# RWKV value and output products over used token rows only, in 32-column array tiles

## The chip, the cores and the metric

The kernel runs on one core of a Trainium2 chip. The metric is the device time of one execution in microseconds (us). TensorE is called PE, its weight loads PEld, VectorE DVE, ScalarE ACT, GpSimd POOL; SP is the engine that issues the transfers.

## The reference

One layer of a hybrid decoder for a prompt of 256 tokens and 8 samples of 4 tokens each (288 columns in all, in fp32), width 2048. One input projection feeds a retention group (8 heads of 256) and an RWKV-7 group (32 heads of 64); both outputs go through one output projection, a gate and the residual, and a final RMSNorm. The change is in the RWKV group, whose recurrence for each head is

```
sa = S @ (-kk_t)
S  = S * w_t + outer(sa, kk_t * a_t) + outer(v_t, k_t)
o_t = S @ r_t
```

Each output `o_t` is normalised over the 64 values of its head, scaled and shifted, a bonus term is added, and the sum is multiplied by a SiLU gate. The state S at the end of the prompt and of each sample is an output too.

## The kernel before

**Order of the work.** The wide matmuls of the projections (tile `acc`, line 419 in `wblocks`) go to PE block by block; each weight block is split into a rounded part `whi` (ACT, line 383) and a remainder `wlo` (DVE or POOL, line 387), three blocks ahead. Everything else is written as generators. A planner at build time keeps an estimated clock for each engine (`account`, line 201, with costs from `c_pe`, `c_dve`, `c_act` and `c_pool`), and after every three wide matmuls `tick` (line 293) lets those generators go on whose inputs its clocks call ready. `flag` and `wait` (lines 322 and 325) order the generators among each other at build time; a generator that waits lets others go ahead of it. The result is one fixed order of instructions for each engine. All instructions of the helper class have line 255 in the profile, so they are told apart by their tiles.

**RWKV groups.** The 32 heads are worked off in 8 groups `q` of four heads: two pairs `p` of two heads `h`. The prompt is cut into 8 chunks of 32 tokens (`CH`), and the 32 sample tokens are a ninth chunk, c = 8. For each group `main_gen` (line 784) does, in this order:

- `AR` (line 806) and `BK` (lines 827 to 833): decayed and scaled rows; AR has the tag "AR" or "BK" in turn, and BK of the last group takes the tag "AR".
- the score product `scp` (line 855): four-tile matmuls `mm4` of 64 x 64, masked into `SC`. In SC, UV and XR the 64 partitions of a head are two halves of 32: in SC and UV the first half stands for the delta rows and the second for the value rows.
- the turn stage (`turn_gen`, line 930): transposes of BK, in which the second half of the tile `UV` serves as scratch, then copies into `BKt`.
- the values are transposed into rows 32 to 63 of each head's part of `UV` (lines 868 to 879).
- the value product `avp` (line 891): for each p, c and head one matmul of 32 rows and 64 columns into two PSUM tiles of the tag "ch" (which has two buffers) and a third for c = 8; ACT brings it into `XR` under the mask `amask` (lines 893 and 894).
- beside it `inv_gen` (line 952) inverts the chunk triangles, and then `chain_gen` (line 1011) goes through the 8 chunks one after the other, adding into XR and filling the first rows of UV; `sample_gen` (line 1077) does chunk 8.
- `out_gen` (line 1132): the output product `ops` (line 1142), 36 matmuls of 64 rows and 64 columns, is added to XR (lines 1145 and 1146); the output rows then stand in 32 of each 64 partitions. Then come 18 statistics instructions over all of XR (line 1151), small sums, a power on POOL (line 1162), subtraction and scaling (lines 1165 and 1169), copies that bring 32 x 32 blocks into place (ACT, lines 1173 and 1177) and a transpose into `on` (line 1179), flag "xr", and the last two steps into the rows `y` of the output projection's input, flag "rw".

An fp32 matmul is two instructions in the profile, one for each pass.

**The end.** After the last group's projections the output projection runs. Its input rows are split in pairs by `split_gen` (line 1502), which waits for "rw" of the last group before its ninth pair (line 1506); the blocks that use these pairs come at a fixed place in the order (line 1569), the first of them 22 blocks after the first output block.

Of the kernel before, what the change touches and what calls it, by code (L numbers as in the profile page):

```python
# [10 lines left out]
F32 = mybir.dt.float32  # L11
F32R = mybir.dt.float32r
AF = mybir.ActivationFunctionType
# [88 lines left out]
def tile_hybrid_step(  # L102
# [222 lines left out]
    def wait(*names):  # L325
        while not all(n in flags for n in names):
            yield
        cur[0].done["flag"] = max(flags[n] for n in names)
        yield
# [358 lines left out]
    def rwkv_blocks(q):  # L688
# [95 lines left out]
        def main_gen():  # L784
# [17 lines left out]
            yield  # L802
            yield from wait(("la", q))
            if q > 1:
                yield from wait(("ops", q - 2))
            ar = mx.tile([P, 2, 9, 2, CH], F32, tag="BK" if q % 2 else "AR", name="AR")
            AR = [ar[:, p] for p in range(2)]
            for p in range(2):
                ep, es = eps_[p]
                stt(AR[p][:, 0:8, 0, :], c9(kkn[p][:, 0:TP]), -1.0, ep[:, :, 0:32], MUL, MUL)  # L810
                stt(bb(AR[p][:, 8, 0, :]), bb(kkn[p][:, TP:NR]), -1.0, es[:, :, 0:4], MUL, MUL)
                yield
# [28 lines left out]
                yield from wait(("ops", q - 1))  # L841
            BKt = mx.tile([P, 2, 9, 64], F32, tag="BKt", name="BKt")
            SC = mx.tile([P, 2, 9, 64], F32, tag="SC", name="SC")
            UV = mx.tile([P, 2, 9, 64], F32, tag="UV", name="UV")
            B.update(AR=AR, BKt=BKt, SC=SC, UV=UV)
            mk = K("mwkv")
            flat = lambda t: t.rearrange("p a t -> p (a t)")
            yield PART
# [16 lines left out]
            spawn(bonus_gen(kps))  # L865
            vw = B["vw"]
            yield from wait(("turn", q))
            V.transpose(UV[:, 0, :, 32:64], c9(vw[:, 0, :]))
            yield
            for h in range(2):  # L870
# [11 lines left out]
            XR = mx.tile([P, 2, 9, 64], F32, tag="XR", name="XR")  # L882
            B["XR"] = XR
            yield PART
            avps, av8 = [pch.tile([P, 512], F32, tag="ch", name="avp") for p in range(2)], tps("avp")
            for p in range(2):
                for c in range(9):
                    for h in hs2:
                        v = slice(h.start + 32, h.stop)
                        t = avps[p][h, 64 * c:64 * c + 64] if c < 8 else av8[h, 64 * p:64 * p + 64]  # L890
                        mm(t, SC[v, p, c, :], UV[v, p, c, :])
            for p in range(2):
                act(XR[:, p, 0:8, :].rearrange("p c k -> p (c k)"), avps[p], AF.Copy, scale=K("amask"))
            act(XR[:, :, 8, :], av8[:, 0:128].rearrange("p (a k) -> p a k", a=2), AF.Copy, scale=K("amask"))
            yield from pace(SPC)
            yield from wait(("inv", q), ("bkt", q))
# [31 lines left out]
            flag(("bps", q))  # L928

        def turn_gen(BK, BKt):  # L930
            T2 = B["UV"][:, 1]
            for a in range(2):
                s = slice(32 * a, 32 * a + 32)
# [197 lines left out]

        def out_gen():
            SC, UV, XR = B["SC"], B["UV"], B["XR"]
            bst = rwp.tile([P, 18, 6], F32, tag="bst", name="bst")
            gst = rwp.tile([P, 3, 18], F32, tag="gst", name="gst")
            yield PART
            ops, op8 = [pch.tile([P, 512], F32, tag="ch", name="ops") for p in range(2)], tps("ops")
            for p in range(2):
                for c in range(9):
                    for h in hs2:  # L1140
                        t = ops[p][h, 64 * c:64 * c + 64] if c < 8 else op8[h, 64 * p:64 * p + 64]
                        mm(t, SC[h, p, c, :], UV[h, p, c, :])
            for p in range(2):
                xv = XR[:, p, 0:8, :].rearrange("p c k -> p (c k)")
                tt(V, xv, ops[p], xv, ADD)
            tt(V, XR[:, :, 8, :], op8[:, 0:128].rearrange("p (a k) -> p a k", a=2), XR[:, :, 8, :], ADD)
            yield from pace(SPC)
            flag(("ops", q))
            for p in range(2):
                for c in range(9):  # L1150
                    V.bn_stats(bst[:, 9 * p + c], XR[:, p, c, :])
                yield
            mean, dif, var = gst[:, 0], gst[:, 1], gst[:, 2]
            tt(V, mean, bst[:, :, 1], bst[:, :, 4], ADD)
# [4 lines left out]
            ts(V, mean, mean, 0.5, None, MUL)  # L1159
            yield  # L1160
            ts(G, var, var, 1.0 / 64, 64e-5, MUL, ADD)
            tt(G, var, var, nhalf[:, 0:18], ALU.pow)
            yield
            for p in range(2):
                tt(V, XR[:, p], XR[:, p], gst[:, 0, 9 * p:9 * p + 9].unsqueeze(2).to_broadcast([P, 9, 64]), SUB)
                yield
            for p in range(2):
                o = XR[:, p]
                tt(V, o, o, gst[:, 2, 9 * p:9 * p + 9].unsqueeze(2).to_broadcast([P, 9, 64]), MUL)
                on = rwp.tile([P, NR], F32, tag="on", name="on")  # L1170
                yield
                for h in range(2):
                    S.copy(o[quad(h, 0), :, 32 - 32 * p:64 - 32 * p], o[quad(h ^ p, 1), :, 0:32])
                yield
                if p == 1:
                    for h in range(2):
                        S.copy(o[quad(h, 1), :, 0:32], o[quad(1 - h, 1), :, 32:64])
                    yield
                V.transpose(c9(on), o[:, :, 32 - 32 * p:64 - 32 * p])
                yield  # L1180
                if p == 1:
                    flag(("xr", q))
                stt(on, on, lnw(p), yd(p), MUL, ADD)
                stt(yd(p), on, lnb(p), sg[:, p], ADD, MUL)
                yield
# [432 lines left out]
```

## Time and profile before

| | us |
|---|---|
| median of three runs | 1561.44 (1560.08 to 1562.62) |
| the profiled execution, its own time | 1563.12 |
| span of its instructions | 1561.3 |
| mean granted clock of PE | 0.973 |

The profile is one execution, taken by the hardware profiler. Its page gives busy time by engine, a groups view lists instructions of equal kind with their count, busy time and mean length, and a timeline has them in order of time; a line of the timeline with "x72" is 72 instructions merged, its length from the first start to the last end. "Idle before" is time in which the engine did nothing just before the instruction, and the name behind the arrow is what it then waited for.

### The profile page before, as it was taken

Reading aid. Unit: us, or ns where it says so; the run is one execution under the profiler, and the core shown is the slowest. Engines: PE = TensorE matmul, PEld = TensorE weight load, DVE = VectorE, ACT = ScalarE, POOL = GpSimd, SP = SyncE. Lnnn points to the kernel's source line nnn. Section 1 sums busy time; section 2 is a strip of 40 time slices with the busy share of each in tenths; the row PEclk is TensorE's granted clock in tenths of the full one; section 3 lists DMA queues with packets and bytes.
Section 4 is the critical chain, followed back from the end, with each engine's and each line's share of the span. In section 5 each row is a group of like instructions: output and inputs, shape, how many; then the busy total and the mean of one; then the engine's idle time right before and its main releaser. Section 6 shows DMA issues by size and latency. Waiting matters only on the chain. (4 is left out here: it accounts for less than half of the span.)

```text
span 1561.3 us, 37454 instructions
## 1 busy us (share of the span) xinstructions
PE 1463.4 (94%) x14194; PEld 1305.5 (84%) x14194; DVE 1165.6 (75%) x2889; ACT 778.4 (50%) x1698; POOL 462.4 (30%) x469
## 2 busy tenths in 40 slices
PE   4889999999999999899999999999999989999996
PEld 1668887888888878888888899879987977999996
DVE  2434787998788878967987799789878987855453
ACT  2224564464445644644555546545653554455443
POOL 0001322442343145323422353245243422202010
PEclk8889999999999999999999999999999999999998
DMA  9996654674476557645764566466536544675553
GB/s 286 341 347 213 196 156 129 183 195 146 126 240 193 146 146 220 189 119 154 216 182 137 154 180 174 114 170 179 155 101 182 159 133 111 193 237 167 158 162 115
DMA packets 347761, 277.30 MB, mean 178 GB/s; under 512 B 90270, under 2 KB 346110, under 8 KB 346868
## 3 DMA queue, kind: packets, MB, share of 16 engines
q1 hardware_dynamic: 347580, 274.91, 60.5%
q8 instruction: 111, 1.82, 0.5%
q14 instruction: 70, 0.57, 0.1%
HBM read 248.80 MB, written 26.03 MB: 176 GB/s over the span
## 5 line engine op out<-in xcount | busy, mean ns | idle before, releaser
L255 PE MATMUL acc<-Hhi,whi 128*128 128x288 f32 (+2 forms) x2080 | 618.6, 312 | 13.3 <-ACT whi L255 5.3
L255 PE MATMUL acc<-Hlo,whi 128*128 128x288 f32 (+2 forms) x2080 | 618.6, 309 | 0.0
L255 ACT CAST whi<-raw 128x512 fp32r<-128x512 f32 (+1 forms) x648 | 395.4, 618 | 353.0 <-PE acc L255 209.2
L255 POOL TENSOR_TENSOR wlo<-raw,whi 128x512 fp32r<-128x512 f32 x224 | 311.0, 1392 | 758.5 <-ACT whi L255 546.0
L255 PE MATMUL acc<-Hhi,wlo 128*128 128x288 f32 (+2 forms) x2080 | 458.5, 302 | 14.8 <-DVE wlo L255 13.9
L255 PEld LDWEIGHTS acc<-Hhi,whi 128*128 128x128 f32 (+1 forms) x2080 | 397.5, 191 | 42.7 <-issue 11.3
L255 PEld LDWEIGHTS acc<-Hlo,whi 128*128 128x128 f32 (+1 forms) x2080 | 398.4, 192 | 17.3 <-issue 8.1
L255 DVE TENSOR_TENSOR wlo<-raw,whi 128x512 fp32r<-128x512 f32 (+1 forms) x424 | 304.8, 724 | 121.7 <-ACT whi L255 117.0
L255 PEld LDWEIGHTS acc<-Hhi,wlo 128*128 128x128 f32 (+1 forms) x2080 | 340.5, 191 | 22.0 <-DVE wlo L255 19.7
L255 PE MATMUL acc<-ylo,whi 128*128 128x288 f32 x480 | 136.4, 298 | 0.7 <-DVE ylo L255 0.7
L255 PE MATMUL acc<-yhi,whi 128*128 128x288 f32 x480 | 135.9, 298 | 1.0 <-ACT whi L255 1.0
L255 PE MATMUL acc<-yhi,wlo 128*128 128x288 f32 x480 | 101.5, 297 | 0.1
L255 PEld LDWEIGHTS acc<-yhi,whi 128*128 128x128 f32 x480 | 90.4, 188 | 1.4 <-ACT whi L255 1.3
L255 PEld LDWEIGHTS acc<-ylo,whi 128*128 128x128 f32 x480 | 90.4, 188 | 1.3 <-DVE ylo L255 1.0
L255 PEld LDWEIGHTS acc<-yhi,wlo 128*128 128x128 f32 x480 | 76.3, 189 | 0.7 <-POOL wlo L255 0.3
L255 PE MATMUL adaps<-raw,cT 128*32 128x256 f32 x768 | 56.3, 409 | 7.8 <-DMA raw<-in_w_ada_dram 7.8
L255 DVE COPY UV<-ch 32x64 f32<-32x64 f32 x128 | 28.9, 225 | 29.1 <-ACT UV L255 26.1
L255 ACT COPY UV<-ch 32x64 f32<-32x64 f32 x128 | 25.5, 199 | 47.8 <-PE ch L255 46.0
L255 DVE SCALAR_TENSOR_TENSOR s0b<-s0b,ups 128x512 f32<-128x512 f32 x64 | 41.0, 681 | 9.0 <-PE ups L255 8.9
L255 PEld LDWEIGHTS adaps<-raw,cT 128*32 128x32 f32 x768 | 20.2, 114 | 30.4 <-DMA raw<-in_w_ada_dram 15.3
L255 POOL TENSOR_TENSOR rot<-rot,rt 128x288 f32<-128x288 f32 x32 | 29.1, 932 | 44.7 <-DVE rt L255 44.7
L255 DVE SCALAR_TENSOR_TENSOR S<-ch,dec,SP 128x64 f32<-128x64 f32 x112 | 30.5, 278 | 13.8 <-PE ch L255 12.7
(260 smaller groups left out, 1966.8 us busy)
## 6 DMA issues: line engine op xcount, KB each, us to landing
raw<-in_w_in_dram SPq DMA_DIRECT2D x512, 256.0 KB, 3.1
raw<-in_w_ada_dram SPq DMA_DIRECT2D x64, 512.0 KB, 8.3
raw<-in_w_out_dram SPq DMA_DIRECT2D x128, 256.0 KB, 3.0
raw<-in_w_ada_dram SPq DMA_DIRECT2D x64, 256.0 KB, 2.8
s0b<-in_state_ret_dram SPq DMA_DIRECT2D x64, 256.0 KB, 4.6
out_dram<-s0b SPq DMA_DIRECT2D x64, 256.0 KB, 3.2
y<-in_x_prompt_dram SPq DMA_DIRECT2D x4, 1024.0 KB, 6.6
s0r<-in_state_rwkv_dram SPq DMA_DIRECT2D x128, 32.0 KB, 2.8
```

What stands on the lines that cost most here:

```text
L255: return f(*a, **k)
```

## The change

The value product and the output product are computed for those 32 of 64 rows of each head that hold a result, so that every matmul writes 32 partitions in place of 64; the odd chunks are written into the neighbouring 32 columns of the array, and with that into the other 32 partitions of the head. The prompt chunks of one product fit in one "ch" tile in place of two. ACT brings the value product into XR with one copy for the odd and one for the even chunks (each under the mask), and two more that move the odd chunks' rows to their place. The sum of ops and XR goes into a new place `O`, the AR tile of the group (for group 6 the UV tile), in which 5 columns of 64 stand on all 128 partitions in place of 9: four pairs of chunks, and the sample chunk on one half. Statistics, power, subtraction and scaling run over these 10 columns instead of 18. Sixteen copies instead of six bring the blocks back into XR for the transpose.

The tiles' owners change with it: AR of group q waits for the flag "xr" of group q-2 in place of "ops"; UV is taken in `turn_gen` in place of `main_gen`, and in the last group only after "xr" of group 6.

```diff
--- before.py
+++ after.py
@@ -802,9 +802,10 @@
             yield
             yield from wait(("la", q))
             if q > 1:
-                yield from wait(("ops", q - 2))
+                yield from wait(("xr", q - 2))
             ar = mx.tile([P, 2, 9, 2, CH], F32, tag="BK" if q % 2 else "AR", name="AR")
             AR = [ar[:, p] for p in range(2)]
+            B["ar"] = ar
             for p in range(2):
                 ep, es = eps_[p]
                 stt(AR[p][:, 0:8, 0, :], c9(kkn[p][:, 0:TP]), -1.0, ep[:, :, 0:32], MUL, MUL)
@@ -841,8 +842,7 @@
                 yield from wait(("ops", q - 1))
             BKt = mx.tile([P, 2, 9, 64], F32, tag="BKt", name="BKt")
             SC = mx.tile([P, 2, 9, 64], F32, tag="SC", name="SC")
-            UV = mx.tile([P, 2, 9, 64], F32, tag="UV", name="UV")
-            B.update(AR=AR, BKt=BKt, SC=SC, UV=UV)
+            B.update(AR=AR, BKt=BKt, SC=SC)
             mk = K("mwkv")
             flat = lambda t: t.rearrange("p a t -> p (a t)")
             yield PART
@@ -865,6 +865,7 @@
             spawn(bonus_gen(kps))
             vw = B["vw"]
             yield from wait(("turn", q))
+            UV = B["UV"]
             V.transpose(UV[:, 0, :, 32:64], c9(vw[:, 0, :]))
             yield
             for h in range(2):
@@ -882,15 +883,20 @@
             XR = mx.tile([P, 2, 9, 64], F32, tag="XR", name="XR")
             B["XR"] = XR
             yield PART
-            avps, av8 = [pch.tile([P, 512], F32, tag="ch", name="avp") for p in range(2)], tps("avp")
-            for p in range(2):
-                for c in range(9):
-                    for h in hs2:
-                        v = slice(h.start + 32, h.stop)
-                        t = avps[p][h, 64 * c:64 * c + 64] if c < 8 else av8[h, 64 * p:64 * p + 64]
-                        mm(t, SC[v, p, c, :], UV[v, p, c, :])
-            for p in range(2):
-                act(XR[:, p, 0:8, :].rearrange("p c k -> p (c k)"), avps[p], AF.Copy, scale=K("amask"))
+            avp, av8 = pch.tile([P, 512], F32, tag="ch", name="avp"), tps("avp")
+            av5 = avp.rearrange("p (a j k) -> p a j k", a=2, j=4)
+            xr5 = XR[:, :, 0:8, :].rearrange("p a (j b) k -> p a j b k", b=2)
+            for p in range(2):
+                for c in range(8):
+                    for x in range(2):
+                        mm4(av5[quad(x, c % 2), p, c // 2], SC[quad(x, 1), p, c, 0:CH], UV[quad(x, 1), p, c, :])
+            for p in range(2):
+                for x in range(2):
+                    mm(av8[hs2[x], 64 * p:64 * p + 64], SC[quad(x, 1), p, 8, :], UV[quad(x, 1), p, 8, :])
+            for b in (1, 0):
+                act(xr5[:, :, :, b], av5, AF.Copy, scale=K("amask"))
+            for x in range(2):
+                S.copy(xr5[quad(x, 0), :, :, 1], av5[quad(x, 1)])
             act(XR[:, :, 8, :], av8[:, 0:128].rearrange("p (a k) -> p a k", a=2), AF.Copy, scale=K("amask"))
             yield from pace(SPC)
             yield from wait(("inv", q), ("bkt", q))
@@ -928,6 +934,9 @@
             flag(("bps", q))
 
         def turn_gen(BK, BKt):
+            if q == 7:
+                yield from wait(("xr", 6))
+            B["UV"] = mx.tile([P, 2, 9, 64], F32, tag="UV", name="UV")
             T2 = B["UV"][:, 1]
             for a in range(2):
                 s = slice(32 * a, 32 * a + 32)
@@ -1131,24 +1140,28 @@
 
         def out_gen():
             SC, UV, XR = B["SC"], B["UV"], B["XR"]
-            bst = rwp.tile([P, 18, 6], F32, tag="bst", name="bst")
-            gst = rwp.tile([P, 3, 18], F32, tag="gst", name="gst")
+            O = UV.rearrange("p a c k -> p a (c k)") if q == 6 else B["ar"].rearrange("p a c x t -> p a (c x t)")
+            O = O[:, :, 0:320].rearrange("p a (j k) -> p a j k", j=5)
+            bst = rwp.tile([P, 10, 6], F32, tag="bst", name="bst")
+            gst = rwp.tile([P, 3, 10], F32, tag="gst", name="gst")
             yield PART
-            ops, op8 = [pch.tile([P, 512], F32, tag="ch", name="ops") for p in range(2)], tps("ops")
+            ops, op8 = pch.tile([P, 512], F32, tag="ch", name="ops"), tps("ops")
+            op5 = ops.rearrange("p (a j k) -> p a j k", a=2, j=4)
+            xr5 = XR[:, :, 0:8, :].rearrange("p a (j b) k -> p a j b k", b=2)
             for p in range(2):
                 for c in range(9):
-                    for h in hs2:
-                        t = ops[p][h, 64 * c:64 * c + 64] if c < 8 else op8[h, 64 * p:64 * p + 64]
-                        mm(t, SC[h, p, c, :], UV[h, p, c, :])
-            for p in range(2):
-                xv = XR[:, p, 0:8, :].rearrange("p c k -> p (c k)")
-                tt(V, xv, ops[p], xv, ADD)
-            tt(V, XR[:, :, 8, :], op8[:, 0:128].rearrange("p (a k) -> p a k", a=2), XR[:, :, 8, :], ADD)
+                    for x in range(2):
+                        t = op5[quad(x, 1 - c % 2), p, c // 2] if c < 8 else op8[quad(x, 1), 64 * p:64 * p + 64]
+                        mm4(t, SC[hs2[x], p, c, CH:], UV[hs2[x], p, c, :])
+            tt(V, O[:, :, 0:4], op5, xr5[:, :, :, 0], ADD)
+            for x in range(2):
+                tt(V, O[quad(x, 0), :, 0:4], op5[quad(x, 0)], xr5[quad(x, 1), :, :, 1], ADD)
+                tt(V, O[quad(x, 1), :, 4], op8[quad(x, 1), 0:128].rearrange("p (a k) -> p a k", a=2), XR[quad(x, 1), :, 8], ADD)
             yield from pace(SPC)
             flag(("ops", q))
             for p in range(2):
-                for c in range(9):
-                    V.bn_stats(bst[:, 9 * p + c], XR[:, p, c, :])
+                for j in range(5):
+                    V.bn_stats(bst[:, 5 * p + j], O[:, p, j])
                 yield
             mean, dif, var = gst[:, 0], gst[:, 1], gst[:, 2]
             tt(V, mean, bst[:, :, 1], bst[:, :, 4], ADD)
@@ -1159,24 +1172,21 @@
             ts(V, mean, mean, 0.5, None, MUL)
             yield
             ts(G, var, var, 1.0 / 64, 64e-5, MUL, ADD)
-            tt(G, var, var, nhalf[:, 0:18], ALU.pow)
-            yield
-            for p in range(2):
-                tt(V, XR[:, p], XR[:, p], gst[:, 0, 9 * p:9 * p + 9].unsqueeze(2).to_broadcast([P, 9, 64]), SUB)
-                yield
-            for p in range(2):
-                o = XR[:, p]
-                tt(V, o, o, gst[:, 2, 9 * p:9 * p + 9].unsqueeze(2).to_broadcast([P, 9, 64]), MUL)
+            tt(G, var, var, nhalf[:, 0:10], ALU.pow)
+            yield
+            for p in range(2):
+                tt(V, O[:, p], O[:, p], gst[:, 0, 5 * p:5 * p + 5].unsqueeze(2).to_broadcast([P, 5, 64]), SUB)
+                yield
+            for p in range(2):
+                tt(V, O[:, p], O[:, p], gst[:, 2, 5 * p:5 * p + 5].unsqueeze(2).to_broadcast([P, 5, 64]), MUL)
                 on = rwp.tile([P, NR], F32, tag="on", name="on")
                 yield
                 for h in range(2):
-                    S.copy(o[quad(h, 0), :, 32 - 32 * p:64 - 32 * p], o[quad(h ^ p, 1), :, 0:32])
-                yield
-                if p == 1:
-                    for h in range(2):
-                        S.copy(o[quad(h, 1), :, 0:32], o[quad(1 - h, 1), :, 32:64])
+                    for i in range(2):
+                        for b in range(2):
+                            S.copy(XR[quad(h, i), p, b::2, 0:32], O[quad(h ^ p, 1 - b), p, 0:5 - b, 32 * i:32 * i + 32])
                     yield
-                V.transpose(c9(on), o[:, :, 32 - 32 * p:64 - 32 * p])
+                V.transpose(c9(on), XR[:, p, :, 0:32])
                 yield
                 if p == 1:
                     flag(("xr", q))
```

## Rows read from the trace of the kernel before

**Rows 1.** The page: span, then busy time, share and instructions of two engines.

```profile
span 1561.3 us, 37454 instructions
...
PE 1463.4 (94%) x14194; PEld 1305.5 (84%) x14194; DVE 1165.6 (75%) x2889; ACT 778.4 (50%) x1698; POOL 462.4 (30%) x469
```

**Rows 2.** Stretches: length, busy PE, PEld, DVE, ACT, POOL, clock, DMA share, GB/s.

```profile
790.00:938.00 148.00, 145.31 (x1478) 130.05 (x1470) 123.35 (x313) 80.31 (x172) 53.22 (x50) 1.00 0.58 163
...
1256.00:1262.00 6.00, 4.60 (x46) 4.48 (x47) 5.66 (x17) 3.86 (x8) 0.80 (x2) 0.50 0.52 167
```

**Rows 3.** Waits of PE: total us, times, longest.

```profile
PE acc L255 <- DVE wlo L255: 13.9, 18, 2.3
```

**Rows 4.** Groups of PE by shape: count, busy us, mean ns, idle before.

```profile
L255 PE MATMUL avp<-UV,SC 32*64 32x64 f32 x576 | 20.2, 226 | 4.1 <-ACT UV L255 4.0
L255 PE MATMUL ops<-UV,SC 64*64 64x64 f32 x576 | 19.6, 227 | 0.0
```

**Rows 5.** Timeline of PE: start us, length us, shape, count of merged instructions.

```profile
789.54 1.28 PE L255 MATMUL scp<-AR,y 64*64 64x64 f32 x72
...
821.65 2.31 PE L255 MATMUL avp<-UV,SC 32*64 32x64 f32 x72
823.90 0.40 PE L255 MATMUL acc<-Hhi,whi 128*128 128x288 f32 x1
...
838.64 0.31 PE L255 MATMUL ch<-XR,WT 32*32 32x64 f32 x8
...
882.39 1.07 PE L255 MATMUL rcr<-s0b,qp 128*32 128x256 f32 x16
...
1315.70 1.03 PE L255 MATMUL rst<-vkt 128*128 128x256 f32 x4
```

**Rows 6.** Groups of DVE, ACT and POOL by shape.

```profile
L255 DVE BATCH_NORM_STATS2 bst<-XR 128x6 f32<-128x64 f32 x144 | 19.6, 209 | 0.0
...
L255 DVE TENSOR_TENSOR UV<-ups,XR 32x128 f32<-32x128 f32 x48 | 13.5, 282 | 0.9
...
L255 DVE TENSOR_TENSOR XR<-ops,XR 128x512 f32<-128x512 f32 x16 | 11.1, 691 | 11.5 <-PE ops L255 11.5
...
L255 ACT COPY UV<-ch 32x64 f32<-32x64 f32 x128 | 25.5, 199 | 47.8 <-PE ch L255 46.0
L255 ACT COPY XR<-XR 32x288 f32<-32x288 f32 x48 | 20.7, 430 | 19.1 <-DVE XR L255 18.5
...
L255 POOL TENSOR_TENSOR gst<-gst,nhalf 128x18 f32<-128x18 f32 x8 | 26.3, 3290 | 0.7
```

**Rows 7.** Timelines of DVE and PE: last groups' stages, group 4's first transpose.

```profile
792.88 0.47 DVE L255 STREAM_TRANSPOSE UV<-y 128x288 f32<-128x288 f32 x1
...
1212.83 2.32 PE L255 MATMUL ops<-UV,SC 64*64 64x64 f32 x72
...
1229.13 0.47 DVE L255 STREAM_TRANSPOSE UV<-BK 128x288 f32<-128x288 f32 x1
...
1253.31 0.48 DVE L255 STREAM_TRANSPOSE on<-XR 128x288 f32<-128x288 f32 x1
...
1257.40 2.19 PE L255 MATMUL avp<-UV,SC 32*64 32x64 f32 x36 [3.23 <-ACT UV L255]
...
1272.61 0.97 PE L255 MATMUL ivb<-WT,itmp 32*16 32x16 f32 x64
...
1276.89 0.31 PE L255 MATMUL ch<-XR,WT 32*32 32x64 f32 x8
```

**Rows 8.** Timelines of DVE and PE where the last rows enter the output projection.

```profile
1363.44 0.52 DVE L255 SCALAR_TENSOR_TENSOR y<-on,pt,y 128x288 f32<-128x288 f32 x1
...
1364.91 0.75 DVE L255 TENSOR_TENSOR ylo<-y,yhi 128x576 fp32r<-128x576 f32 x1
...
1371.33 0.29 PE L255 MATMUL acc<-yhi,whi 128*128 128x288 f32 x1
```

## The prediction

> **What bounds the kernel now.** I read the page's engine table first: TensorE (PE) is busy for 94% of the span, VectorE (DVE) for 75% [rows 1]. An average can mix stages, so the stretches come next: in the stretch of head group 4 PE is busy 145.31 of 148 us, DVE 123.35, ScalarE (ACT) 80.31, at a granted clock of 1.00 [rows 2]. The waits of PE say the same from the other side: the kind that adds up to most, a wide matmul waiting for the DVE half of a split weight block, comes to 13.9 us in 18 times [rows 3]. So a microsecond of matmul taken out of the PE queue should be a microsecond of span, unless a new wait takes its place.
>
> **Two products made cheaper on PE.** Per head group the kernel runs the value product (avp) and the output product (ops) as 36 fp32 matmuls each, 72 instructions each since fp32 takes two passes; 8 groups give the 576 of either [rows 4]. In the timeline avp's burst takes 2.31 us for 72 instructions [rows 5], and ops has the same count and nearly the same busy time; less some 0.22 us of the last instruction, that is 2.09/71 = 29.4 ns from start to start. Only two array tiles alternate in them, one for each half of the array, so a pair takes 59 ns. The score product (scp), 72 instructions of the same 64 columns over four different tiles, takes 1.28 us: (1.28 - 0.22)/71 = 14.9 ns, so four tiles go by in 60 ns [rows 5]. The step from two tiles to four is what the change makes: the new products write 32 partitions each, and even and odd chunks land in neighbouring column quarters. Of the 72 passes, 64 go by fours (16 waves instead of 32) and the 8 of the sample chunk stay in pairs (4 waves). So 16 waves of 58.8 ns go away in each burst: 0.94 us. No row shows the new shapes in a long burst; the nearest is the chain's 32x32 product, whose four tiles are two row quarters by four column quarters, exactly avp's new layout: (0.31 - 0.21)/7 = 14 ns [rows 5]. I take the scp price for both. The value burst now changes tile shape once inside, from 32 to 64 columns for the sample chunk. A change of shape is visible where avp gives way to the wide matmuls: the last avp instruction starts at 821.65 + 2.31 - 0.22 = 823.74 and the wide one 0.16 us later, at 823.90 [rows 5], where the next of its kind would have come within 0.06. So I charge 0.1 us, with ends of 0 and 0.25. Sum: 2 x 0.94 - 0.1 = 1.78 us for a head group, 14.2 us for eight.
>
> One thing speaks against: the new bursts put all four tiles into one PSUM bank, while scp and the chain's product write two banks. The rows answer in two steps. Avp as it is writes one bank from two row quarters; if these took turns, each pass would cost what a lone one costs. A lone fp32 pass of 256 columns takes (1.03 - 0.38)/3 = 217 ns, so 64 columns would take about 54 ns, not 29.4 [rows 5]. And four column quarters write one bank together in rcr, 16 passes of 256 columns: (1.07 - 0.38)/15 = 46 ns each [rows 5]. So the four-tile price stands. The Trainium skill, TensorEngine Tiling (Array Packing), Restrictions and Gotchas, says that tiles in different rows of the array cannot use the same PSUM bank at the same time. By that rule the sum above would be nought; the trace of avp does not agree with it.
>
> **The other engines, per head group.** DVE: the evacuation of ops was two adds of 0.69 us and one of 0.28; it becomes one add of 512 columns on all partitions, two of 512 columns on 32 partitions and two of 128. Cost goes with columns, not partitions, so +0.69 + 0.28 = +0.97 us. The statistics fall from 18 to 10 at 19.6/144 = 0.136: -1.09. The four passes of subtract and scale go from 576 to 320 columns; between the 128-column row at 0.282 and the 512-column row at 0.691 a column costs 1.07 ns, so -0.27 each, -1.09 [rows 6]. Together -1.2 us, some 10 us in all. POOL: the power over 18 elements takes 3.29 us, over 10 then 1.83: -1.46 us of pure latency [rows 6]. ACT: the two masked copies of avp stay, and two 32-partition copies of 512 columns come on top. Between 0.199 us at 64 and 0.430 at 288 columns a column costs 1.03 ns, so +0.66 each. The six rearranging copies of 0.430 become sixteen of 160 or 128 columns at 0.30 and 0.27: 4.5 for 2.6 us [rows 6]. Together +3.2 us (end: copies with short runs that cost as much as the old 0.43, +5.6), 26 us in all. With ACT at 80.31 of 148 us [rows 2] there is room; it is hidden beside matmuls because weight casts run ahead, and I charge nothing. Its price without cover: the eight copies of one half now stand in ACT's queue as one run of 2.3 us ahead of the next weight cast, sixteen times, so at worst a few us of PE in all.
>
> **Waits moved.** The scaled rows (AR) of group q now wait for the end of normalisation of q-2 instead of its output product, since the output is written into AR. In group 6 normalisation ends 41 us after its output product starts (1212.8 to 1253.8), while the value bursts of groups 4 and 7 end 435.6 us apart (823.96 and 1259.59), 145 us a group [rows 5, 7]: it is long over. In the last group a true wait comes in: its turn stage can't have the UV tile before normalisation of group 6 is over. Behind it stand four DVE transposes, eight ACT copies, the value copies, avp and the serial chain. Before, that stage starts at 1229.13 and the last transpose of normalisation is at 1253.31 to 1253.8 [rows 7], so it starts 24.7 us later. Part of that is slack. In group 4 the value burst starts 28.8 us after the first transpose (792.88 to 821.65) [rows 5, 7]; here it would start at 1253.8 + 28.8 = 1282.6 and the chain, 1.3 us of burst and some 3 us of copies later, at 1287, against 1276.89 now, when it only follows the inverse that ends at 1273.6 [rows 7]. That is 10 us late, less about 3 us by which the shorter normalisation of group 6 ends sooner (1.46 of power, the rest DVE): 7 us. At the end the last group's rows are finished at 1363.96 and their split at 1365.66, and the first output block that needs the space comes at 1371.33 [rows 8]: 5.7 us of slack, plus 3 us from the last group's own shorter normalisation. So 8.7 covers 7, barely; I charge 1 us. What can be gained there is larger than that: PE now stands 3.23 us for the value copies of that group [rows 7] and then runs at half the clock, 1.2 GHz (granted 0.50 from 1256 to 1262) [rows 2], so up to 3.2 + 3 us could go, if the later burst no longer meets the copies.
>
> **Sum.** The profiled execution spans 1561.3 us [rows 1] of its own 1563.12; the median of the three runs is 1561.4, 1.7 lower, and I take the difference to it: 1561.4 - 14.2 + 1.0 = 1548.2, say 1548.
>
> **Rivals.**
> - *Paid back in waits.* PE no longer binds alone and the stretch follows DVE, at 83% of group 4 [rows 2]. Then only DVE's own 10 us come back: about 1552, with ACT's longer runs up to 1558. For it: the waits on split weights are the longest kind of PE wait [rows 3]. Against it: 24 us of idle DVE in that stretch.
> - *The tiles don't run together.* Tiles of two row groups that write one bank, or two column quarters fed by one row group, have to take turns: waves stay pairs, bursts stay 2.3 us, and the time is 1561. Against it: the chain's 32x32 product and rcr [rows 5]. The Trainium skill's rule on banks (TensorEngine Tiling (Array Packing), Restrictions and Gotchas) is this rival's first form.
> - *Slower: the last group's wait.* If none of the 24.7 us is absorbed, the output projection stands still for 24.7 - 8.7 = 16 us, and a stop of 3.23 us already brought 6 us of half clock, 3 us lost [rows 2, 7]: 1561.4 - 14.2 + 19 = 1566. It decides from a delay of about 23 us on at the first block that needs the late rows; the chain's present slack behind the inverse speaks against it.
>
> **How the numbers follow.** Forecast 0.66 (1539 to 1552; the low end has the stall of the last group gone, 14.2 + 6.2 = 20.4, and no mode charge or shorter waits for 2 more), paid back 0.16 (1552 to 1558), no gain 0.10 (1558 to 1564), slower 0.08. A measurement can tell about 0.2%, 3.1 us, from no change, so the bounds are 1558.3 and 1564.5: faster 0.82, same 0.10, slower 0.08. The range 1539 to 1558 leaves the last two and little else out.
>
> **What would show it.** Right: avp and ops bursts of 72 in about 1.3 us, their groups at some 11 us each; the power at 1.8 us; 80 statistics; DVE some 10 us lower and ACT some 26 higher; matmul groups of the projections unchanged. Wrong: bursts still 2.3 us long; idle PE after long ACT runs; idle PE of over 3 us between 1240 and 1370 with half clock behind it, above all before the output block that needs the last group's rows.

## The result, and the profile after

The change made the kernel slower: 1573.35 us (median of five runs, 1569.08 to 1579.52) against 1561.44 of the kernel before in the same rounds (five runs, 1558.49 to 1562.62). The ratio is 1.0076, 95% interval 1.0052 to 1.0101. The forecast was 1548, with 1558 as the upper end. Times of one kernel spread over 3 to 13 us from one execution to the next, so the verdicts below go by ratios to the kernel before in the same rounds, with 95% intervals (a ratio is taken over all runs and is not quite the quotient of two medians), and single traces only show where time sits.

The page of the changed kernel, beside [rows 1]:

```profile
span 1571.6 us, 37510 instructions
...
PE 1460.5 (93%) x14194; PEld 1294.9 (82%) x14194; DVE 1156.5 (74%) x2864; ACT 806.4 (51%) x1794; POOL 424.7 (27%) x446
```

DVE is 9.1 us less busy and ACT 28.0 us more, as forecast. PE is only 2.9 us less busy. Its groups by shape show that the two products themselves did what was forecast (first operation, shape and count, then busy us, mean ns of one, idle before):

```profile
L255 PE MATMUL ops<-UV,SC 64*32 64x64 f32 x576 | 10.5, 218 | 0.0
L255 PE MATMUL avp<-UV,SC 32*32 32x64 f32 x512 | 8.8, 216 | 0.0
```

Beside [rows 4], ops fell from 19.6 to 10.5 us and avp from 20.2 to 8.8 and 3.6 for its sample chunk. Against that stand longer waits of PE (total us, times, longest), on splits 21.1 us against 13.9 of [rows 3]:

```profile
PE acc L255 <- DVE wlo L255: 21.1, 20, 2.7
PE acc L255 <- ACT whi L255: 15.0, 14, 2.1
```

The second kind was less than half of that before:

```profile
PE acc L255 <- ACT whi L255: 6.3, 8, 1.0
```

In all, PE idles 111.1 us of the span (span less busy time) against 97.9 before, and its mean granted clock is 0.969 against 0.973. The groups of DVE, ACT and POOL by shape, beside [rows 6]:

```profile
L255 DVE BATCH_NORM_STATS2 bst<-AR 128x6 f32<-128x64 f32 x70 | 10.1, 212 | 0.0
L255 DVE TENSOR_TENSOR AR<-ops,XR 32x512 f32<-32x512 f32 x14 | 9.6, 684 | 0.3
...
L255 ACT COPY XR<-AR 32x160 f32<-32x160 f32 x56 | 18.2, 325 | 16.0 <-DVE AR L255 15.2
L255 ACT COPY XR<-AR 32x128 f32<-32x128 f32 x56 | 16.7, 298 | 0.7
L255 ACT ACTIVATE XR<-avp,cst 128x512 f32<-128x512 f32 x16 | 10.1, 685 | 9.9 <-PE avp L255 9.9
L255 ACT COPY XR<-avp 32x512 f32<-32x512 f32 x16 | 9.3, 579 | 0.2
...
L255 POOL TENSOR_TENSOR gst<-gst,nhalf 128x10 f32<-128x10 f32 x8 | 15.8, 1971 | 0.7
```

The fourteen 32x512 adds and the sixteen 32x512 copies are the longer evacuation, the 112 small copies the new rearrangement (two more adds and sixteen more copies, those of group 6, stand under another tile's name). The names to keep for what follows: **burst** is one of the sixteen stretches of avp or ops on PE, **evacuation** the copies and adds that take its sums out of PSUM.

### The profile page after: what moved, and what is told of

It is laid out like the page before. It is cut to its first block, busy times and chain, and to the rows that moved or that the text cites. A ratio compares the mean times of both kernels' runs of the same rounds, so it can differ in the third digit from the quotient of the medians.

```text
span 1571.6 us, 37510 instructions
## 1 busy us (share of the span) xinstructions
PE 1460.5 (93%) x14194; PEld 1294.9 (82%) x14194; DVE 1156.5 (74%) x2864; ACT 806.4 (51%) x1794; POOL 424.7 (27%) x446
## 5 line engine op out<-in xcount | busy, mean ns | idle before, releaser
L255 POOL TENSOR_TENSOR wlo<-raw,whi 128x512 fp32r<-128x512 f32 x201 | 276.2, 1377 | 798.5 <-ACT whi L255 530.7
L255 PE MATMUL acc<-Hhi,wlo 128*128 128x288 f32 (+2 forms) x2080 | 460.5, 303 | 24.1 <-DVE wlo L255 21.1
L255 DVE TENSOR_TENSOR wlo<-raw,whi 128x512 fp32r<-128x512 f32 (+1 forms) x447 | 329.4, 741 | 142.0 <-ACT whi L255 136.4
L255 ACT COPY XR<-AR 32x160 f32<-32x160 f32 x112 | 34.8, 311 | 16.6 <-DVE AR L255 15.2
```

The source lines that it names most:

```text
L255: return f(*a, **k)
```

## Experiments

Three theories stood. **Order**: the planner, told other costs, issues everything else in a worse order. **Side work**: the longer evacuation and the sixteen copies hold up the weight casts and splits or the PSUM buffers. **Paid back**, the prediction's first rival: the burst was cover for other engines, and a shorter one only uncovers them. Most kernels below are written so that the planner is told the old costs; each engine's order is then that of the kernel before but for the instructions added, changed or left out, so two traces can be compared matmul by matmul. Idle PE below is always the span less PE's busy time.

**1. Order against instructions.** The first kernel has the new instructions in the old order (group 6 keeps its old output stage, so that the last group needs no new wait):

```diff
+            mute[0] = True
             op5 = ops.rearrange("p (a j k) -> p a j k", a=2, j=4)
...
+            mute[0] = False
+            for _ in range(36):
+                account("PE", 0.085)
+            for n in (512, 512, 128):
+                account("DVE", (n / 0.96 + 62) * 1e-3)
```

> The changed products, sums, statistics and copies, put into the order of the kernel before: the planner is told the old costs and steps, and group 6 keeps its old output stage, so no new wait comes in and every other instruction of every engine stands where it stood. If the new order lost the time: about 1548 us (1545 to 1551), seven eighths of the forecast gain. If the new ACT copies and DVE sums themselves hold up the weight splits: 1560 or more. If the last group's wait alone lost it: 1548 as well.

Measured: 1575.67, ratio 1.0061 (1.0039 to 1.0082): most of the loss comes without the new order. The second kernel has the old instructions in exactly the order of the changed kernel:

> The old products, sums and copies, put into the order of the changed kernel, its wait in the last group's turn stage with it. If the new order lost the time: about 1587 us (1573 plus the 14 of the bursts), 1580 at least. If the new instructions themselves did: near 1561.

Measured: 1568.6, ratio 1.0035 (1.0021 to 1.0049), between the two expectations. The third takes over only the two new waits, that of AR and that of the last group:

```diff
-                yield from wait(("ops", q - 2))
+                yield from wait(("xr", q - 2))
...
+            if q == 7:
+                yield from wait(("xr", 6))
+            B["UV"] = mx.tile([P, 2, 9, 64], F32, tag="UV", name="UV")
```

> The kernel before with one thing of the change: the last group's turn stage waits in the planner for the normalisation of group 6 before it takes UV. If that wait is what cost the time: 1575 or more. If it costs only what stands after 1260 us in the changed trace: 1564 to 1568. If the slack covers it, as forecast: 1561 to 1563.

Measured: 1567.83, ratio 1.0023 (1.0012 to 1.0034). Its trace has the order of the kernel before up to 1229 us, so the last group's wait it is: the wide matmuls start 1.5 us later than their counterparts before at 1211 us, and 5.1 later from 1402 on. The fourth gives each weight split of the changed kernel back to the engine that had it before (224 on POOL instead of 201):

> The changed kernel, but each weight block's remainder is computed on the engine that the kernel before used for it (224 on POOL in place of 201). If the loss is DVE work that the planner moved off POOL: 1555 to 1562. If it is the order at large: 1568 to 1576, as the changed kernel.

Measured: 1581.93, ratio 1.0116 (1.0091 to 1.014), above both expectations: the planner's new choice of engines was rather a help than the harm. So the order by itself accounts for about half of the loss, and the larger part of that is the last group's wait. The waits of PE on splits that stood out in the changed kernel's trace are the order's all the same: the second kernel, with old instructions, has them too, the first, nearly as slow as the change, much less. In the waits on casts the two differ little (10.2 and 8.9 us).

```profile
PE acc L259 <- DVE wlo L259: 20.2, 20, 2.9
...
PE acc L259 <- ACT whi L259: 10.2, 10, 2.2
```

(old instructions, new order), and in the first kernel (new instructions, old order):

```profile
PE acc L259 <- DVE wlo L259: 15.7, 20, 2.5
...
PE acc L259 <- ACT whi L259: 8.9, 11, 1.2
```

The rest has to be found in the instructions. Against the kernel before, the first kernel's bursts are shorter by 0.84 us (avp) and 1.00 us (ops) each, some 13 in all, but idle PE grows from 97.9 to 111.6 us, and PE is busy only 0.8 us less: the matmuls outside the bursts take some 12 us longer, at a mean granted clock of 0.965 in place of 0.973.

**2. One term at a time.** The fifth kernel is the one before with nothing but shorter bursts:

```diff
-                        mm(t, SC[h, p, c, :], UV[h, p, c, :])
+                        if c % 2 == 0:
+                            mm(t, SC[h, p, c, :], UV[h, p, c, :])
```

> The kernel before, every instruction of VectorE, ScalarE and GpSimd kept in kind, size and order; on TensorE the odd chunks of both products are left out (their copies and adds read the even chunks twice), so each burst loses 32 of its 72 passes, 32 x 29.4 ns = 0.94 us, what the new tiles save. 'The burst's gain is real and the side work eats it' expects 2 x 8 x 0.94 = 15 us less: 1547 against 1562 of before (ratio 0.989 to 0.993). 'Paid back' (the bursts were cover for weight splits, and what they lose comes back as waits just behind) expects at most 4 us less: 1558 to 1563, with PE gaps and half clock up by 10 us or more.

Measured: 1558.16 against 1563.32, ratio 0.9966 (0.995 to 0.9983). Its timeline has the burst, its waits the split:

```profile
816.38 1.38 PE L259 MATMUL avp<-UV,SC 32*64 32x64 f32 x40
```

```profile
PE acc L259 <- DVE wlo L259: 18.2, 22, 2.5
```

The burst of 2.31 us [rows 5] is 0.93 shorter, the sixteen together 15 us; 5 arrive (3 to 8 by the interval). The wait on splits rose from 13.9 [rows 3] to 18.2 us with nothing added on any engine. How the other 10 were lost is shown only in part: in this trace, one of the faster runs (1555.13), 8 of the 15 arrive, idle PE grows by 3.1 us in all and the matmuls outside the bursts take 3.9 longer, less than the 10 that *paid back* expected. The counterpart issues each matmul of both products twice:

> The kernel before with its order; every matmul of both products is issued twice, 2.1 us more of TensorE in each of the sixteen bursts, 34 us in all, all other engines the same. 'TensorE sets the pace' expects +34 us: 1597. 'Paid back' works in this direction too if the bursts are cover (a longer burst gives the weight splits a start and shortens the waits behind it): +18 to +28 us, 1581 to 1591.

Measured: 1590.88 against 1564.25, ratio 1.0175 (1.0156 to 1.0193). 34 us of PE work cost 27, idle PE fell from 97.9 to 90.0 us, and the wait on splits fell below that of [rows 3]:

```profile
PE acc L259 <- DVE wlo L259: 11.8, 15, 2.5
```

So a microsecond of burst was worth about a third of one when taken out (0.2 to 0.5 by the interval), and about 0.8 when put in. Next, the longer evacuation alone, on the kernel before:

```diff
+            for p in range(2):
+                S.copy(XR[quad(0, 0), p, 0:8, :]..., avps[p][quad(0, 0)])
...
+            for p in range(2):
+                xv = XR[quad(0, 0), p, 0:8, :]...
+                tt(V, xv, ops[p][quad(0, 0)], xv, ADD)
```

> The kernel before with its order, and only the longer evacuation added: behind the two value copies two more ScalarE copies of 32x512 (0.66 us each), behind the two output adds two more VectorE adds of 32x512 (0.69 us each), in all eight groups, on rows that the result does not use or that hold the same values. The engines are busy 11 us more each. 'The extra evacuation is the cost' expects +8 to +12 us: 1571 to 1575 against 1563. 'It only costs where the bursts no longer cover it' (the cost needs the shorter bursts) expects +0 to +4: 1563 to 1567.

Measured: 1574.98 against 1564.25, ratio 1.0065 (1.0041 to 1.0089). DVE is busy 11.2 us longer and ACT 6.4, and the time grows by about 10, although DVE idles a quarter of the time. In its trace, 13.6 us longer than that of the kernel before, only 2.8 us is idle PE; the same matmuls take 10.8 us longer, at a mean granted clock of 0.967 in place of 0.973. Then the small copies alone:

> The kernel before with its order; the six rearranging copies of 32x288 in a group are cut into sixteen of 32x160 and 32x128 (four of them twice). ScalarE +2.3 us a group, 18 us in all. 'The small copies hold up the weight casts' expects +4 to +6 us: 1567 to 1569. 'ScalarE has room, they hide' (the step of the prediction that charged nothing) expects no change: 1562 to 1565.

Measured: 1569.47, ratio 1.0035 (1.0019 to 1.005). The prediction's "I charge nothing" was worth 5 us. The three terms, -0.34, +0.65 and +0.35%, sum to +0.66%, beside 0.61% measured for all new instructions in that order.

**3. The parts from the other side.** The value product alone, the output product alone, and both without the extra evacuation:

> Order of before; the value product in the new tiles with its two extra copies of 32x512 on ScalarE (1.3 us a group), output stage as before in all groups. Side work eats it: bursts -7.5 us in all; the longer evacuation (about 1.3 us later, eight times) keeps the chain and the weight casts waiting: 1560 to 1566. Rearranging copies are to blame (they are not in here): 1554. Paid back: 1560 to 1563.

> Order of before; the value product as before, the output product, its five adds and the new normalisation with sixteen small copies in groups 0 to 5 and 7. Rearranging copies or the longer evacuation are to blame: most of the 11.7 us that all new instructions together cost in this order are here, 1568 to 1575. Value product to blame: 1556 to 1562. Paid back: 1561 to 1565.

> All new instructions in the order of before (as in the first experiment), without the two extra value copies on ScalarE and without the two 32x512 adds on VectorE (left out: the odd chunks of half the partitions of both products). Extra evacuation to blame (it holds the PSUM buffers and the queues): back to 1555 to 1562. Rearranging copies to blame: stays at 1569 to 1575. Paid back: 1564 to 1570.

> The output product alone as in the seventh experiment (1572.8 there, ratio 1.0055), without its two 32x512 adds on VectorE (left out: the odd chunks of half the partitions). Adds to blame: ratio 1.000 to 1.001, 1563 to 1565. Sixteen copies to blame: 1.004 to 1.006, 1569 to 1573.

Measured: value product 1.0013 (0.9998 to 1.0027), output product 1.0055 (1.0037 to 1.0072), both without the extra evacuation 0.9997 (0.9982 to 1.0013), output product without its extra adds 0.9987 (0.9973 to 1.0001). The value product decides little, as its bands overlap; the third, at 1562.9, lies between its bands; the second and the fourth together put the cost on the adds. The output product is the dear half, and two adds of 0.68 us in seven groups, 9.6 us of DVE, make the whole difference between 1.0055 and 0.9987, some 10 us. One PSUM tile in place of two, without these adds, loses nothing; that the single tile costs by itself is not shown.

**4. Why an add costs its whole length.** Here is the output burst of group 2 and what follows, PE and DVE, in the kernel before (start us, length us, operation, count, idle before):

```profile
597.34 2.31 PE L255 MATMUL ops<-UV,SC 64*64 64x64 f32 x72
...
600.58 0.50 PE L255 MATMUL ups<-kv 32*128 32x256 f32 x4
...
598.53 0.69 DVE L255 TENSOR_TENSOR XR<-ops,XR 128x512 f32<-128x512 f32 x1 [0.91 <-PE ops L255]
599.58 0.89 DVE L255 TENSOR_TENSOR XR<-ops,XR 128x512 f32<-128x512 f32 x2 [0.36 <-PE ops L255]
```

DVE takes the first half out while PE still works on the second. In the first experiment's kernel the burst is one PSUM tile and half as long; all five adds come after it, the sample chunk's two among and behind the large ones:

```profile
601.20 1.31 PE L259 MATMUL ops<-UV,SC 64*32 64x64 f32 x72
...
603.44 0.38 PE L259 MATMUL ups<-kv 32*128 32x256 f32 x1
605.36 0.47 PE L259 MATMUL ups<-kv 32*128 32x256 f32 x3 [1.54 <-DVE AR L259]
...
602.48 2.73 DVE L259 TENSOR_TENSOR AR<-ops,XR 128x512 f32<-128x512 f32 x5
```

Three `ups` matmuls (a product of the retention group) wait 1.54 us for a buffer of the pool `tp`, which the sample chunk's add releases last. What that brings on stands in the stretch behind it (length, busy PE, PEld, DVE, ACT, POOL, clock, DMA share, GB/s):

```profile
604.00:616.00 12.00, 10.64 (x66) 10.23 (x67) 8.85 (x27) 3.38 (x6) 7.22 (x6) 0.86 0.54 151
```

The granted clock is 0.86 over these 12 us, as part of them runs at 1.2 instead of 2.4 GHz; in the kernel before, the 12 us from 600 on have 1.00. The thirteenth kernel puts the two small adds first and changes nothing else:

```diff
+            for x in range(2):
+                tt(V, O[quad(x, 1), :, 4], op8[...], XR[quad(x, 1), :, 8], ADD)
             tt(V, O[:, :, 0:4], op5, xr5[:, :, :, 0], ADD)
             for x in range(2):
                 tt(V, O[quad(x, 0), :, 0:4], ...)
-                tt(V, O[quad(x, 1), :, 4], op8[...], XR[quad(x, 1), :, 8], ADD)
```

> The first experiment's kernel (new instructions, order of before; ratio 1.0061) with the two 128-column adds of the sample chunk put ahead of the three 512-column adds; nothing else moves. 'The adds hold the PSUM buffer that the next sample product waits for': the two waits of 1.9 us behind the output burst and the half clock after them go, 4 to 7 us less: ratio 1.002 to 1.004, 1567 to 1570. 'VectorE's time itself is the cost': unchanged, 1.005 to 1.007.

Measured: 1567.19, ratio 1.0028 (1.0018 to 1.0039). The `ups` wait is gone, and the clock of the stretch with it:

```profile
599.40 1.31 PE L259 MATMUL ops<-UV,SC 64*32 64x64 f32 x72
...
601.63 0.50 PE L259 MATMUL ups<-kv 32*128 32x256 f32 x4
```

```profile
602.00:614.00 12.00, 12.00 (x91) 11.62 (x88) 11.85 (x41) 5.83 (x11) 9.49 (x11) 1.00 0.65 188
```

About 5 of the 9.5 us (the two intervals just meet) were thus the PSUM buffer's order of release. Over the whole trace idle PE stays at 111.5 us, but PE is busy 7.3 us less, at a mean granted clock of 0.971 against 0.965: in these two traces the gain is in the clock. Another stall stays in the first and in this kernel, here in the first, behind the output burst of group 1 (start 435.73):

```profile
437.00 2.72 DVE L259 TENSOR_TENSOR AR<-ops,XR 128x512 f32<-128x512 f32 x5 [0.94 <-PE ops L259]
...
442.31 0.76 DVE L259 TENSOR_TENSOR_SCAN la<-keep,t 128x288 f32<-128x288 f32 x1
...
443.10 0.42 ACT L259 ACTIVATE ep<-la 128x256 f32<-128x256 f32 x1 [2.58 <-DVE la L259]
...
445.31 0.37 PE L259 MATMUL acc<-Hhi,whi 128*128 128x296 f32 x1 [1.94 <-DVE kw L259]
```

The scan starts 6.6 us after the burst's start, in place of 4.1 before (432.09 to 436.23): the adds end 0.9 us later than they did, and what stands between them and the scan takes 1.6 us longer, which the adds do not explain. ACT waits 2.58 us for the scan with the evacuation of `acc` (kw) behind it, DVE's part of that comes late, and PE has no buffer for 1.94 us. Before, PE did not wait for DVE there. Both stalls go with the two 32x512 adds: in the traces of the first kernel and of the output product alone PE waits 3.1 us for the adds at `ups` and 2.3 for kw, in the two kernels of part 3 that leave these adds out not at all and 0.5. The same two small adds put first in the changed kernel itself:

> The changed kernel with the same two adds put first, order otherwise the same. Buffer held: 3 to 7 us less than the changed kernel, ratio 1.003 to 1.006. VectorE's time itself: unchanged, ratio 1.007 to 1.009.

Measured: 1572.95, ratio 1.0075 (1.0051 to 1.0099): no gain is seen, though the interval's lower end still touches the expected band. In the changed kernel's order `ups` stood for that buffer only 0.6 us in all; its waits sit elsewhere, at weight splits and casts. One of them, ACT of the changed kernel (a run of copies between two casts):

```profile
1271.09 0.62 ACT L255 CAST whi<-raw 128x512 fp32r<-128x512 f32 x1
...
1273.10 1.34 ACT L255 COPY MR<-zt 32x256 f32<-32x256 f32 x2
1274.45 2.14 ACT L255 COPY WT<-zt 32x512 f32<-32x512 f32 x2
1276.61 0.62 ACT L255 CAST whi<-raw 128x512 fp32r<-128x512 f32 x1
```

and PE, which stood until that cast was done, with the clock of the 4 us after it:

```profile
1277.28 0.61 PE L255 MATMUL acc<-Hhi,whi 128*128 128x288 f32 x1 [2.14 <-ACT whi L255]
```

```profile
1277.00:1281.00 4.00, 3.72 (x16) 3.72 (x17) 2.85 (x4) 3.90 (x9) 1.11 (x1) 0.57 0.31 76
```

These copies are old ones, and the kernel before has them in one piece ahead of a cast too:

```profile
1263.28 0.63 ACT L255 CAST whi<-raw 128x512 fp32r<-128x512 f32 x1 [0.34 <-PE acc L255]
1266.03 1.33 ACT L255 COPY MR<-zt 32x256 f32<-32x256 f32 x2 [2.12 <-DVE zt L255]
1267.38 2.19 ACT L255 COPY WT<-zt 32x512 f32<-32x512 f32 x2
1269.59 1.14 ACT L255 CAST whi<-raw 128x512 fp32r<-128x512 f32 x2
```

There no cast came for 5.7 us, in the new order for 4.9, and yet PE waited for a cast only in the new order. So the run of copies alone does not make the stall; why the casts were less far ahead of PE is not shown.

**5. The terms taken off.** The fifteenth kernel keeps the new products and normalisation in the old order, but GpSimd fills the zeros of the value rows and shifts the odd chunks' sums to the rows where the output product lands (the sample chunk's output product is back in 64-column tiles, with one add):

```diff
-            for b in (1, 0):
-                act(xr5[:, :, :, b], av5, AF.Copy, scale=K("amask"))
+            act(xr5[:, :, :, 0], av5, AF.Copy, scale=K("amask"))
...
+                for x in range(2):
+                    G.tensor_copy(xr5[quad(x, 0), :, :, 0], xr5[quad(x, 1), :, :, 1])
...
+            tt(V, O[:, :, 4], op8[...], XR[:, :, 8], ADD)
             tt(V, O[:, :, 0:4], op5, xr5[:, :, :, 0], ADD)
-            for x in range(2):
-                tt(V, O[quad(x, 0), :, 0:4], op5[quad(x, 0)], xr5[quad(x, 1), :, :, 1], ADD)
...
```

> The first experiment's kernel with less evacuation: the zeros of the value rows come from two GpSimd fills (one ScalarE copy of 128x512 less), GpSimd shifts the odd chunks' sums onto the rows where the output product lands once the chain is done (the two 32x512 adds on VectorE go), and the sample chunk is one add, put first. Per group VectorE -1.7, ScalarE -0.65 us against the first experiment, GpSimd four operations of 32x512 more. 'The three terms are the cause': burst gain -5, copies +5, one extra ScalarE copy +1 to +2, VectorE 2.5 us a group below before: ratio 0.997 to 1.001, 1559 to 1566. If something else of the new instructions costs: above 1.003.

Measured: 1566.02, ratio 1.0023 (1.0003 to 1.0044), with the expected band reached only by the lower end of its interval: the three terms may not be the whole cost. The sixteenth also gives eight of the sixteen small copies to GpSimd, the seventeenth all; the eighteenth is the sixteenth again in other rounds:

```diff
-                            S.copy(XR[quad(h, i), p, b::2, 0:32], O[...])
+                            (G.tensor_copy if i == h else S.copy)(XR[quad(h, i), p, b::2, 0:32], O[...])
```

> As the kernel before this one, and eight of the sixteen small copies on GpSimd. ScalarE -2.4 us a group. 'The copies cost because they stand in ScalarE's queue ahead of weight casts': 2 to 4 us less than the kernel before this one: ratio 0.994 to 0.999, 1555 to 1562. 'GpSimd's own weight splits are then late': 1.000 or more.

> As the sixteenth experiment with all sixteen small copies on GpSimd (0.44 us each there against 0.31 on ScalarE, so one group's take 7 us, in which GpSimd's weight splits of 1.38 us wait). 'The copies' place in ScalarE's queue is their cost': another 1 to 3 us less, ratio 0.995 to 0.998, 1556 to 1560. 'GpSimd's weight splits are then late': 1.000 or more, 1564 or more.

> The kernel of the sixteenth experiment again, for a tighter interval: 0.997 to 0.999, 1558 to 1562 where before has 1563.

Measured: 1561.42, ratio 0.9981 (0.997 to 0.9993); all sixteen 1568.16, ratio 1.0015 (0.9999 to 1.0031); the repetition 1560.62 against 1565.66, ratio 0.9974 (0.9961 to 0.9987). The groups of POOL and ACT in the sixteenth:

```profile
L259 POOL COPY XR<-AR 32x160 f32<-32x160 f32 x28 | 13.1, 467 | 27.4 <-DVE AR L259 26.7
...
L259 ACT COPY XR<-AR 32x160 f32<-32x160 f32 x28 | 9.1, 323 | 12.8 <-DVE AR L259 12.4
```

A copy is slower on POOL (467 against 323 ns) and the kernel faster by about 0.4%; PE's wait on casts falls from 8.7 to 6.5 us and idle PE from 107.7 to 102.7. What counts here is the queue in which a copy stands, and shared between two queues the copies cost least. That "GpSimd's weight splits are then late" with all sixteen there was argued ahead of the run and fits its time, but PE's wait on them did not grow (1.1 us against 1.7), so it is not shown. The version with half of the copies on GpSimd is below both kernels: a fifth to a quarter of a per cent below the one before.

## Why the prediction failed, step by step

- **Bursts, 16 waves of 58.8 ns, and 0.1 us for the change of shape**: right. In the changed kernel's trace a burst takes 1.47 (avp) and 1.31 us (ops) in place of 2.31. The rule on banks that the prediction weighed against the row does not hold in this trace: four tiles of two row groups in one bank ran together, 10.5 us for 576 passes. The rival *The tiles don't run together* falls.
- **"A microsecond of matmul taken out of the PE queue should be a microsecond of span"**: this step failed. 15 us taken out alone gave 5 (3 to 8). The proviso "unless a new wait takes its place" was the case, though what took its place is shown only in part (3.1 us of idle PE and 3.9 of slower matmuls, part 2). PE's 145.31 busy of 148 us showed who is busy, not that the others were ahead of it; the waits on splits [rows 3] were the warning, and they grew.
- **DVE, -1.2 us a group**: the sum is right (9.1 us less busy), the reading wrong. The saving (statistics, subtract, scale) brought nothing that the runs show: all new instructions without the extra evacuation give 0.9997, and the bursts' -0.34 and the copies' +0.35% make as much without it. The extra 1 us stands at the release of PSUM, where PE waits. It was charged by busy time and not by place. The idle 11.5 us before the old adds [rows 6] show that DVE was ahead of the burst and took its first half while PE worked on the second; one tile ends that, which the prediction did not weigh. With ACT's part the extra evacuation cost about 10 us.
- **ACT, +26 us, "hidden beside matmuls"**: size right (28.0), cover wrong. The small copies alone cost 5 us, though they came in runs of four and not eight. The prediction's "at worst a few us" was their true price.
- **POOL's power**: 1.97 us against 1.83 forecast, of no weight.
- **The last group's wait, charged 1 us**: 3.6 measured alone (0.23%). The delay was about twice the working's: the 3 us by which the normalisation of group 6 was to end sooner did not come (43.5 us from the start of its output product, against 41 before), the turn stage starts 4.4 us after its last transpose, the value burst 25.5 after that, and the chain at 1291.16, 14.3 us later than before, where the working had 10 less 3:

```profile
1254.70 0.48 DVE L255 STREAM_TRANSPOSE on<-XR 128x288 f32<-128x288 f32 x1
1259.58 0.48 DVE L255 STREAM_TRANSPOSE UV<-BK 128x288 f32<-128x288 f32 x1
...
1285.07 1.47 PE L255 MATMUL avp<-UV,SC 32*32 32x64 f32 x72
...
1291.16 0.31 PE L255 MATMUL ch<-XR,WT 32*32 32x64 f32 x8
...
1378.68 0.40 PE L255 MATMUL acc<-yhi,whi 128*128 128x288 f32 x1 [1.24 <-ACT yhi L255]
```

  The stop at the first late output block is 1.24 us and another of 0.60 follows; the 16 us of the rival *the last group's wait* did not come. With the two waits alone, in the third kernel's trace, idle PE is as before (97.9 us) and the same matmuls take 5.2 us longer, at a mean granted clock of 0.971 against 0.973.
- **Rivals**: *Paid back in waits* named the mechanism of the burst's loss, but gave it only DVE's own 10 us as a gain. The case that came true, extra evacuation worth more than the burst, was not among them. The Trainium skill, TensorEngine Tiling (Array Packing), PSUM Bottleneck, says that tiling speeds up TensorE and not the emptying of PSUM, which can then become the limit. It would have been the rival to price; here the trace agrees with it, 2.73 us of adds behind a burst of 1.31.

The sum in ratios: burst -0.34, evacuation +0.65, copies +0.35, the new order with its wait +0.35% (alone) make +1.01%, where 0.76% (0.52 to 1.01) was measured. The parts' intervals are wide enough for that; how much the order costs beside the new instructions is not settled beyond it.

## What to carry to other kernels

A busy engine's time is worth its length only if what runs beside it is ahead; test that by cutting its work alone before rewriting a stage for it. Charge an added copy or add by where it stands (which PSUM buffer it holds, which cast or scan is behind it in the queue), not by the idle share of its engine. Evacuate first the small tile whose buffer the next product wants (about 5 us in one order here, no gain seen in the other), and spread small copies over queues rather than let them stand in the queue that feeds the bound engine.

## What the runs showed of the hardware

- Half clock about doubled the price of two stalls: over the 12 us that begin within the 1.54 us wait of `ups`, the granted clock was 0.86, (1 - 0.86) x 12 = 1.7 us more; behind the 2.14 us wait on a cast it was 0.57 over 4 us, again 1.7. With only the longer evacuation added, idle PE grew by 2.8 us, and the same matmuls took 10.8 us longer at a mean granted clock of 0.967 in place of 0.973.
- In the sixteenth kernel a copy of 32x160 takes 323 ns on ACT and 467 on POOL; one of 32x288 (430 [rows 6]) cut into 160 and 128 columns makes 323 + 296 on ACT.
- Tiles of 32x32 and of 64x32 run at the same pace here: 8.8 us for 512 passes and 10.5 for 576, 17 and 18 ns each, the last pass of a burst counted at its whole length.
